# Key stores behind the first queries, exponents behind the taps, and a product on GpSimd in a two-layer hybrid encoder

## The chip, the cores and the metric

The kernel runs on one core of one Trainium2 chip. The time is the device time of one execution in microseconds (us). A core has five engines, each with its own instruction queue: PE (TensorE, matmuls; PEld is its weight load), DVE (VectorE), ACT (ScalarE), POOL (GpSimd) and SP (SyncE, which in this kernel only issues DMAs). An engine works through its queue in order, and an instruction that waits for a semaphore holds up everything behind it on its engine. L12 means line 12 of the kernel before the change.

## The reference

A trunk of two layers on 512 tokens with 1024 channels, in float32. Each layer adds half a SwiGLU block, a mixer, half a second SwiGLU block, and a gated embedding. The mixer of layer 0 is a bidirectional Mamba-2 scan (SSD), that of layer 1 a two-dimensional neighbourhood attention.

```python
for i in range(DEPTH):                                   # DEPTH = 2
    h = h + 0.5 * swiglu(rmsnorm(h, ffn1_norm[i]), ...)
    hn = rmsnorm(h, mix_norm[i])
    h = h + (ssd_mixer(hn, ...) if i % 2 == 0 else neighbourhood_attention(hn, ...))
    h = h + 0.5 * swiglu(rmsnorm(h, ffn2_norm[i]), ...)
    gate = sigmoid(rmsnorm(h, ple_norm[i]) @ ple_w_gate[i])
    h = h + gate * rmsnorm(p[i] @ ple_w_proj[i], ple_post_norm[i])

def ssd_mixer(h, ...):
    z, xbc, dt_raw = split(h @ w_in)
    xbc = silu(centred_depthwise_conv(xbc, conv_w, conv_b))      # 5 taps over the tokens
    xs, b_f, c_f, b_b, c_b = split(xbc)                          # forward and backward B, C
    dt = softplus(dt_raw + dt_bias)
    y = ssd_scan(forward) + flip(ssd_scan(flipped)) + xs * d_skip
    return rmsnorm(y * silu(z), norm_g) @ w_out

def ssd_scan(x, dt, a, b_mat, c_mat):                            # chunks of 128 tokens
    cum = cumsum(dt * a)
    scores = (c_mat . b_mat) * exp(lower triangle of cum[q] - cum[k])
    ...
```

In the attention, queries and keys are normalised per head, a block of 16 columns of queries sees a window of keys with a bias added, and the softmax weighs the values.

## The kernel before

Activations stay in SBUF, channels on the 128 partitions and tokens along the row (512 columns). A float32 product is made of three faster ones: each operand is split into a rounded high part and a residue, and `gemm` issues high by high (L278), activation residue or weight residue by high (L281, L282), in groups of three for each of the eight 128-channel blocks, 24 matmuls for one unit of 128 output channels. A weight unit comes by DMA into a `wr` tile, ACT casts it to `wh` (L221) and DVE makes its residue `wl` (L223). The tile framework's scheduler orders the instructions of each engine from the program and its own estimates, so an edit in one place can move instructions of others. `tc.issue_after(x)` keeps what stands under it behind instruction x.

**SSD** (`ssd`). First the eight normalised tiles `xn` are made: a product of the residual tile `hk[k]`, the gain and the row factor `R` (L687), and its split into high part and residue (L689, which ends in L303 on ACT and L304 on DVE; with a gain it would be L306 and L307). `project` then runs eight units for each of the eight groups of heads. The first three units of group 0 don't wait for `xn`: they use the unscaled tiles and multiply by R behind (L748). Each of the first six units of a group goes through `conv` (L742 to L760): one tap on ACT (L752), four on DVE (L756), a tanh on ACT (L759) and a last product on DVE (L760). `steps` (L690 to L739) makes the time steps and their cumulants, in which L716 on PE waits for L712 on DVE, and stores the cumulants as rows `crow` and `vrow` in HBM by sixteen small DMAs (L738, L739). `expo` (L789 to L805) loads a row of `crow` to all partitions and makes a tile of exponents with four Relus (L800) and four Exps (L803) on ACT. `scan` transposes and copies the group's inputs (L833), makes the products of C and B for both directions (`dr` 0 and 1; L841), masks them on DVE (L844), multiplies them by the exponents on POOL (L818, L821) and goes on to the outputs of a chunk and across chunks (L906, L909, L926, L929). While the scan of one group runs, the projection of the next does. PSUM has five banks for gemms (`mm_bank`) and three for the others (`px_bank`). Three exponent tiles of group 0 are issued right after its projection:

```python
e0 = [expo(0, j) for j in range(3)]
```

**Attention** (`attention`). Heads come in eight pairs. `keys` projects, normalises and splits the keys of four pairs at a time. A pair's keys are wanted "stacked": high part and residue of one head over one another. For pairs 0 and 1 this is done by DMAs from the split tile at once (`stack`, L1122: two DMAs each, four a pair); the others' keys go to HBM first (`kd`, L1189) and are stacked when their pair comes up. `project(j)` loads the pair's bias (L1204, L1205), projects the queries (L1212), splits them (L1216 on ACT, L1217 on DVE), stacks them by four DMAs (L1224), and makes the norms and the values (L1231, L1234, L1239). `attend(j)` makes the scores (L1255) from the stacked queries and keys, eight matmuls for half of the query blocks, adds the bias (L1265), takes exponents (L1272), and weighs the values (L1289, L1298, L1309). Pair 0's queries are projected while the keys of pairs 0 to 3 still go through normalisation and split.

```python
if js[0] + i < 2:
    stacked[js[0] + i] = [stack(kn.bitcast(F32), a) for a in range(2)]
    kz.append(None)
else:
    kd = dp.tile([P, 2, T], F32, name=nm("kd"))
    sy.dma_start(out=kd, in_=kn.bitcast(F32))
    kz.append(kd)
```

Of the kernel before, what the change touches and what calls it, by code (L numbers as in the profile page):

```python
# [14 lines left out]
P = 128  # L15
T = 512
# [54 lines left out]
def trunk(ctx, tc, A, out):  # L71
# [55 lines left out]
    def col(i):  # L127
        return cst[:, i:i + 1]
# [525 lines left out]
    def ssd(norm, nxt):  # L654
# [30 lines left out]
        for k in range(KD):  # L685
            t = t2()
            v.scalar_tensor_tensor(out=t, in0=hk[k], scalar=col(norm.gain + k), in1=R, op0=ALU.mult, op1=ALU.mult)  # L687
            xn.append(md(F32R))
            split(xn[k], t, None)  # L689

# [54 lines left out]
        def conv(src, ct, dst, raw):  # L745
# [5 lines left out]
            w = lambda j: ccw[:, j * 48 + ct:j * 48 + ct + 1]  # L751
            s.activation(out=a, in_=src, func=AF.Identity, scale=w(2), bias=ccw[:, 240 + ct:241 + ct])  # L752
            for j in (0, 1, 3, 4):
# [38 lines left out]
        def expo(gi, j):  # L792
# [12 lines left out]
            return e  # L805

        def scan(gi, bt, ct_, xt, zt, e0):

# [4 lines left out]
            def need(n):  # L813
                while len(es) <= min(7, n + (gi == 0)):
                    es.append(expo(gi, len(es)))

# [21 lines left out]
            for dr in range(2):  # L838
                pt = px_bank()
                for c in range(NC):  # L840
# [192 lines left out]
        for i, cur in enumerate(project(0)):  # L1033
            if i == 2:
                steps()
        e0 = [expo(0, j) for j in range(3)]

# [8 lines left out]
        for gi in range(NG):  # L1046
# [13 lines left out]
            for i, r in enumerate(beside):  # L1060
                cur = r
                while pending:

                    with tc.issue_after((row_cast if gi == NG - 1 else copied)[0].ins):
# [3 lines left out]
                        else:  # L1068
                            pending.pop(0)()

                for _ in range(count(gi, i)):
                    next(sn, None)
# [36 lines left out]
    def attention(norm, nxt):  # L1109
# [9 lines left out]
        def stack(src, a):  # L1119
            kt = md(F32R)  # L1120
            for x in range(2):
                sy.dma_start(out=kt[x * 64:(x + 1) * 64].bitcast(F32), in_=src[a * 64:(a + 1) * 64])  # L1122
            return kt

        def keys(js):
# [50 lines left out]
            for i in range(4):  # L1176
# [6 lines left out]
                split(kn, rb, None)  # L1183
                if js[0] + i < 2:
                    stacked[js[0] + i] = [stack(kn.bitcast(F32), a) for a in range(2)]
                    kz.append(None)
                else:
                    kd = dp.tile([P, 2, T], F32, name=nm("kd"))
                    sy.dma_start(out=kd, in_=kn.bitcast(F32))  # L1189
                    kz.append(kd)  # L1190
                if js[0]:
# [9 lines left out]
        def project(j):  # L1201
# [17 lines left out]
            for a in range(2):  # L1219
                r_ = slice(a * 64, (a + 1) * 64)  # L1220
                qt = bp.tile([P, T], F32R, name=nm("hs"), tag="hs", bufs=8)
                for x in range(2):
                    c_ = slice(x * 64, (x + 1) * 64)
                    sy.dma_start(out=qt[c_].bitcast(F32), in_=qs[x][r_].bitcast(F32))  # L1224
                qk.append((qt, stacked[j][a] if j < 2 else stack(kz[j], a)))
            yield
# [324 lines left out]
```

## Time and profile before

| | |
|---|---|
| Time, median of 3 runs (lowest to highest) | 2320.96 us (2320.68 to 2321.33) |
| Profiled execution: its own time | 2320.42 us |
| Profiled execution: its span, first to last instruction | 2318.6 us |
| Mean granted TensorE clock over the span | 0.998 of full speed |
| POOL busy | 324.3 us, 14% of the span |
| Data moved by DMA | 281.71 MB, 121 GB/s on average |

The profile is that of one execution. Its page gives the busy time of each engine, the chain of work that ended last, and the costliest groups of instructions; the trace behind it can be asked for the waits of an engine (who waited, for what, how long), for a timeline of single instructions, and for the busy time of each engine in chosen stretches. Idle time of an engine that nobody waits for costs nothing. In this span the SSD mixer's first group lies between about 360 and 480 us and the first attention pair between about 1700 and 1750 us.

### The profile page before, as it was taken

Reading aid. Unit: us, or ns where it says so; the run is one execution under the profiler, and the core shown is the slowest. Engines: PE = TensorE matmul, PEld = TensorE weight load, DVE = VectorE, ACT = ScalarE, POOL = GpSimd, SP = SyncE. Lnnn points to the kernel's source line nnn. Section 1 sums busy time; section 2 is a strip of 40 time slices with the busy share of each in tenths; the row PEclk is TensorE's granted clock in tenths of the full one; section 3 lists DMA queues with packets and bytes.
Section 4 is the critical chain, followed back from the end, with each engine's and each line's share of the span. In section 5 each row is a group of like instructions: output and inputs, shape, how many; then the busy total and the mean of one; then the engine's idle time right before and its main releaser. Section 6 shows DMA issues by size and latency. Waiting matters only on the chain.

```text
span 2318.6 us, 35451 instructions
## 1 busy us (share of the span) xinstructions
PE 2295.0 (99%) x13732; PEld 2026.4 (87%) x13732; DVE 1827.6 (79%) x2621; ACT 1178.5 (51%) x2038; POOL 324.3 (14%) x261
## 2 busy tenths in 40 slices
PE   9999999999999999999999999999989999999999
PEld 7899998788888888999998889999868888999987
DVE  7878868787788958987885898787569859878856
ACT  5434445777677764444445443444437654444452
POOL 0000001254455641000003100000210010000020
PEclk9999999999999999999999999999999999999999
DMA  5323323444444543333223233322457732333232
GB/s 187 118 77 109 105 88 130 136 164 138 145 138 152 185 159 118 105 103 103 100 74 104 101 107 100 101 89 83 166 169 207 222 117 95 110 105 101 84 94 73
DMA packets 105225, 281.71 MB, mean 121 GB/s; under 512 B 13136, under 2 KB 14032, under 8 KB 105056
## 3 DMA queue, kind: packets, MB, share of 16 engines
q1 hardware_dynamic: 104768, 279.30, 36.7%
q8 instruction: 108, 1.77, 0.3%
q14 instruction: 61, 0.50, 0.1%
q10 hardware_dynamic: 288, 0.14, 0.0%
HBM read 259.70 MB, written 13.40 MB: 118 GB/s over the span
## 4 chain that ended last, share of the span: by engine, by line
PE 92%; DVE 4%; ACT 1%; DMA 1%; issue 0%; SPq 0%; POOL 0%; ACTq 0%; DVEq 0%; POOLq 0%
PE ps L278 18%; PE ps L281 18%; PE ps L282 18%; PE ps L510 10%; PE ps L509 10%; PE ps L508 10%; PE ps L926 1%; DVE wl L223 1%; PE ps L885 1%; PE ps L1255 1%; DVE t L756 1%; PE ps L906 1%; PE ps L1309 1%; PE ps L1298 1%; PE ps L841 1%; DVE md L304 1%
## 5 line engine op out<-in xcount | busy, mean ns | idle before, releaser
L278 PE MATMUL ps<-md,wh 128*128 128x512 f32 (+1 forms) x2032 | 799.3, 394 | 1.1 <-DVE t L756 1.1
L282 PE MATMUL ps<-md,wl 128*128 128x512 f32 (+1 forms) x2032 | 790.8, 389 | 1.2 <-DVE wl L223 1.2
L281 PE MATMUL ps<-md,wh 128*128 128x512 f32 (+1 forms) x2032 | 791.7, 390 | 0.0
L221 ACT CAST wh<-wr 128x1024 fp32r<-128x1024 f32 (+2 forms) x395 | 351.7, 892 | 499.9 <-PE ps L281 258.5
L223 DVE TENSOR_TENSOR wl<-wr,wh 128x1024 fp32r<-128x1024 f32 (+2 forms) x395 | 418.2, 1060 | 84.4 <-ACT wh L221 82.7
L282 PEld LDWEIGHTS ps<-md,wl 128*128 128x128 f32 x2032 | 381.9, 188 | 83.2 <-DVE wl L223 2.7
L278 PEld LDWEIGHTS ps<-md,wh 128*128 128x128 f32 x2032 | 382.7, 188 | 75.6 <-issue 2.4
L281 PEld LDWEIGHTS ps<-md,wh 128*128 128x128 f32 x2032 | 382.8, 188 | 71.6
L221 ACT CAST wh<-md 128x1024 fp32r<-128x1024 f32 x175 | 183.6, 1049 | 321.8 <-PE ps L509 299.7
L332 POOL TENSOR_TENSOR sq<-sq,sq 128x512 f32<-128x512 f32 x71 | 101.0, 1423 | 1645.6 <-ACT sq L328 1641.2
L510 PE MATMUL ps<-sc,wl 128*128 128x256 f32 x980 | 277.4, 283 | 0.8 <-DVE wl L223 0.8
L508 PE MATMUL ps<-sc,wh 128*128 128x256 f32 x980 | 276.9, 283 | 0.8 <-ACT wh L221 0.8
L509 PE MATMUL ps<-md,wh 128*128 128x256 f32 x980 | 277.4, 283 | 0.1
L510 PE MATMUL ps<-md,wl 128*128 128x256 f32 x980 | 277.3, 283 | 0.0
L509 PE MATMUL ps<-sc,wh 128*128 128x256 f32 x980 | 277.3, 283 | 0.0
L508 PE MATMUL ps<-md,wh 128*128 128x256 f32 x980 | 277.1, 283 | 0.0
L514 DVE TENSOR_TENSOR t<-ps,t 128x512 f32<-128x512 f32 x245 | 165.9, 689 | 138.4 <-PE ps L510 137.8
L223 DVE TENSOR_TENSOR wl<-md,wh 128x1024 fp32r<-128x1024 f32 x175 | 213.5, 1220 | 16.6 <-ACT wh L221 16.3
L508 PEld LDWEIGHTS ps<-sc,wh 128*128 128x128 f32 x980 | 187.7, 192 | 4.9 <-ACT wh L221 1.0
L509 PEld LDWEIGHTS ps<-sc,wh 128*128 128x128 f32 x980 | 187.7, 192 | 3.9
L509 PEld LDWEIGHTS ps<-md,wh 128*128 128x128 f32 x980 | 188.0, 192 | 1.6 <-DVE md L472 0.4
L508 PEld LDWEIGHTS ps<-md,wh 128*128 128x128 f32 x980 | 188.0, 192 | 1.3
(209 smaller groups left out, 2898.3 us busy)
## 6 DMA issues: line engine op xcount, KB each, us to landing
wr<-in_w_gw_dram SPq DMA_DIRECT2D x70, 512.0 KB, 3.5
md<-in_w_gw_dram SPq DMA_DIRECT2D x70, 512.0 KB, 4.6
wr<-in_w_in_dram SPq DMA_DIRECT2D x65, 512.0 KB, 3.5
wr<-in_w_dn_dram SPq DMA_DIRECT2D x128, 256.0 KB, 2.6
wr<-in_w_gu_dram SPq DMA_DIRECT2D x32, 512.0 KB, 3.6
hs<-crow SPq DMA_DIRECT2D x64, 256.0 KB, 3.6
wr<-in_w_dn_dram SPq DMA_DIRECT2D x32, 384.0 KB, 3.0
wr<-in_w_qkv_dram SPq DMA_DIRECT2D x24, 512.0 KB, 3.7
```

Source lines behind the costliest of these rows:

```text
L221: splits.append(s.copy(out=hi[:, :n], in_=raw[:, :n]))
L223: v.tensor_sub(out=lo[:, :n], in0=raw[:, :n], in1=hi[:, :n])
L278: m = te.matmul(out=pt, lhsT=hi[:, sl], rhs=part(xp, 0, cols), start=first and k == 0, stop=False)
L281: te.matmul(out=pt, lhsT=hi[:, sl], rhs=part(xp, 1, cols), start=False, stop=False)
L282: gemm.last = te.matmul(out=pt, lhsT=lo[:, sl], rhs=part(xp, 0, cols), start=False, stop=last and k == n - 1)
L304: split.low = v.tensor_sub(out=dst[:, 1, :], in0=src, in1=dst[:, 0, :])
L332: (v if fast else g).tensor_add(out=self.acc, in0=self.acc, in1=q)
L508: te.matmul(out=o, lhsT=hi[:, sl], rhs=xh, start=j == 0 and kk == 0, stop=False)
L509: te.matmul(out=o, lhsT=hi[:, sl], rhs=xl, start=False, stop=False)
L510: te.matmul(out=o, lhsT=lo[:, sl], rhs=xh, start=False, stop=j == 1 and kk == 3)
L514: v.tensor_add(out=k[to], in0=pt, in1=k[other])
L756: v.scalar_tensor_tensor(out=a[:, lo:hi], in0=src[:, lo + o:hi + o], scalar=w(j), in1=a[:, lo:hi], op0=ALU.mult, op1=ALU.add)
```

## The change

It has four edits. In `ssd` the product for `xn` goes to POOL without the gain, and the split applies the gain. Of group 0's exponent tiles only the first is issued at once; the others are issued one at a time, each behind the latest ACT tap of `conv`. The C and B product of direction 0 takes a bank of the gemms' pool, in all groups. In `attention` the stacks of pair 1 and the stores of the keys of pairs 2 and 3 are put off until the first pair's query DMAs are issued.

```diff
@@ ssd
             t = t2()
-            v.scalar_tensor_tensor(out=t, in0=hk[k], scalar=col(norm.gain + k), in1=R, op0=ALU.mult, op1=ALU.mult)
+            g.tensor_mul(out=t, in0=hk[k], in1=R)
             xn.append(md(F32R))
-            split(xn[k], t, None)
+            split(xn[k], t, col(norm.gain + k))
@@ conv
-            s.activation(out=a, in_=src, func=AF.Identity, scale=w(2), bias=ccw[:, 240 + ct:241 + ct])
+            conv.tap = s.activation(out=a, in_=src, func=AF.Identity, scale=w(2), bias=ccw[:, 240 + ct:241 + ct])
@@ ssd
+        def spaced(j):
+            with tc.issue_after(conv.tap.ins):
+                return expo(0, j)
+
@@ scan
             def need(n):
                 while len(es) <= min(7, n + (gi == 0)):
-                    es.append(expo(gi, len(es)))
+                    es.append(spaced(len(es)) if gi == 0 else expo(gi, len(es)))
...
             for dr in range(2):
-                pt = px_bank()
+                pt = (mm_bank, px_bank)[dr]()
@@ ssd
-        e0 = [expo(0, j) for j in range(3)]
+        e0 = [expo(0, 0)]
...
+                if gi == 0 and i == 1:
+                    e0.append(spaced(1))
                 for _ in range(count(gi, i)):
                     next(sn, None)
@@ attention
+        unlaid = []
+
+        def lay(j, kn):
+            if j < 2:
+                stacked[j] = [stack(kn.bitcast(F32), a) for a in range(2)]
+            else:
+                kz[j] = dp.tile([P, 2, T], F32, name=nm("kd"))
+                sy.dma_start(out=kz[j], in_=kn.bitcast(F32))
@@ keys
-                if js[0] + i < 2:
-                    stacked[js[0] + i] = [stack(kn.bitcast(F32), a) for a in range(2)]
-                    kz.append(None)
+                j = js[0] + i
+                kz.append(None)
+                if j == 0 or j > 3:
+                    lay(j, kn)
                 else:
-                    kd = dp.tile([P, 2, T], F32, name=nm("kd"))
-                    sy.dma_start(out=kd, in_=kn.bitcast(F32))
-                    kz.append(kd)
+                    unlaid.append((j, kn))
@@ project
-                qk.append((qt, stacked[j][a] if j < 2 else stack(kz[j], a)))
+                qk.append((qt, stacked.get(j, [None] * 2)[a] or stack(kz[j], a)))
+            while unlaid:
+                lay(*unlaid.pop(0))
             yield
```

Three places show what it moves. The first is SP's queue at the first attention pair, before the change. L1122 are the stacks of pairs 0 (`md_16576`) and 1 (`md_16589`), L1189 the stores of keys, L1204 the bias and L1224 the stacking of the queries (`hs_16693`, `hs_16694` are their high part and residue).

```order
L1122 DMA md_16579<-md_16576 64x1024 x2
L1122 DMA md_16582<-md_16576 64x1024 x2
L1122 DMA md_16592<-md_16589 64x1024 x2
L1122 DMA md_16595<-md_16589 64x1024 x2
L1189 DMA kd_16605<-md_16602 128x1024
L1189 DMA kd_16614<-md_16611 128x1024
L1204 DMA md_16654<-in_bias_dram 128x1024
L1224 DMA hs_16697<-hs_16693 64x512
L1224 DMA hs_16697<-hs_16694 64x512
L1224 DMA hs_16700<-hs_16693 64x512
L1224 DMA hs_16700<-hs_16694 64x512
```

With the change the same queue reads as follows; lines are those of the changed kernel (L1128 stacks, L1138 stores, L1218 bias, L1238 queries).

```order
L1128 DMA md_16579<-md_16576 64x1024 x2
L1128 DMA md_16582<-md_16576 64x1024 x2
L1218 DMA md_16644<-in_bias_dram 128x1024
L1238 DMA hs_16687<-hs_16683 64x512
L1238 DMA hs_16687<-hs_16684 64x512
L1238 DMA hs_16690<-hs_16683 64x512
L1238 DMA hs_16690<-hs_16684 64x512
L1128 DMA md_16693<-md_16589 64x1024 x2
L1128 DMA md_16696<-md_16589 64x1024 x2
L1138 DMA kd_16699<-md_16596 128x1024
L1138 DMA kd_16701<-md_16603 128x1024
```

The four query DMAs moved ahead of the four stack DMAs of pair 1 and the two key stores.

The second place is DVE's queue in the front of SSD, up to the weight residue `wl_3916` of the fourth unit that uses `xn`; L708 and L709 belong to the time steps, the others to `conv`. Before the change:

```order
L708 SCALAR_TENSOR_TENSOR sc_3814<-sc_3814,sc_3813 128x256
L748 TENSOR_TENSOR t_3795<-ps_3764,rt_3648 128x512
L760 SCALAR_TENSOR_TENSOR md_3707<-t_3761,t_3755 128x512
L708 SCALAR_TENSOR_TENSOR sc_3814<-sc_3814,sc_3813 128x256
L756 SCALAR_TENSOR_TENSOR t_3797<-t_3795,ccw,t_3797 128x510
L709 SCALAR_TENSOR_TENSOR sc_3814<-sc_3814,sc_3812 128x256
L756 SCALAR_TENSOR_TENSOR t_3797<-t_3795,ccw,t_3797 128x511
L223 TENSOR_TENSOR wl_3916<-wr_3727,wh_3914 128x1024
```

And with the change:

```order
L748 TENSOR_TENSOR t_3795<-ps_3764,rt_3648 128x512
L760 SCALAR_TENSOR_TENSOR md_3707<-t_3761,t_3755 128x512
L708 SCALAR_TENSOR_TENSOR sc_3814<-sc_3814,sc_3813 128x256
L756 SCALAR_TENSOR_TENSOR t_3797<-t_3795,ccw,t_3797 128x510
L708 SCALAR_TENSOR_TENSOR sc_3814<-sc_3814,sc_3813 128x256
L756 SCALAR_TENSOR_TENSOR t_3797<-t_3795,ccw,t_3797 128x511
L708 SCALAR_TENSOR_TENSOR sc_3814<-sc_3814,sc_3813 128x256
L756 SCALAR_TENSOR_TENSOR t_3797<-t_3795,ccw,t_3797 128x511
L708 SCALAR_TENSOR_TENSOR sc_3814<-sc_3814,sc_3813 128x256
L756 SCALAR_TENSOR_TENSOR t_3797<-t_3795,ccw,t_3797 128x510
L708 SCALAR_TENSOR_TENSOR sc_3814<-sc_3814,sc_3813 128x256
L223 TENSOR_TENSOR wl_3916<-wr_3727,wh_3914 128x1024
```

All four taps (L756) of the unit whose bank is `ps_3764` now stand ahead of the residue, and the last step of the time-step polynomial (L709) behind it.

The third place is PE's queue around the cumulants (L716, L721, L733) of the time steps; `ps_3993` and `ps_4027` are the fourth and fifth unit that use `xn`. Before the change the cumulants stand in the fifth unit:

```order
L282 MATMUL ps_3993<-md_3703,wl_3916 128x512
L282 MATMUL ps_4027<-md_3668,wl_3956 128x512
L278 MATMUL ps_4027<-md_3673,wh_3954 128x512
L281 MATMUL ps_4027<-md_3673,wh_3954 128x512
L716 MATMUL ps_3833<-md_3659,msk 128x128 x4
L721 MATMUL ps_3840<-md_3659,ones_t 128x256
L282 MATMUL ps_4027<-md_3673,wl_3956 128x512
L733 MATMUL ps_3851<-msk,md_3659 128x128 x2
```

With the change they stand in the middle of the fourth:

```order
L278 MATMUL ps_3993<-md_3683,wh_3914 128x512
L281 MATMUL ps_3993<-md_3683,wh_3914 128x512
L282 MATMUL ps_3993<-md_3683,wl_3916 128x512
L716 MATMUL ps_3833<-md_3659,msk 128x128 x4
L721 MATMUL ps_3840<-md_3659,ones_t 128x256
L278 MATMUL ps_3993<-md_3688,wh_3914 128x512
L281 MATMUL ps_3993<-md_3688,wh_3914 128x512
L733 MATMUL ps_3851<-msk,md_3659 128x128 x2
L282 MATMUL ps_3993<-md_3688,wl_3916 128x512
```

The cumulants moved up by seventeen rows of PE's queue.

## The prediction

> **What bounds the kernel now.** I began with the page: its span, its busy shares and the summary of the chain that ended last.
>
> ```profile
> span 2318.6 us, 35451 instructions
> PE 2295.0 (99%) x13732; PEld 2026.4 (87%) x13732; DVE 1827.6 (79%) x2621; ACT 1178.5 (51%) x2038; POOL 324.3 (14%) x261
> PE 92%; DVE 4%; ACT 1%; DMA 1%; issue 0%; SPq 0%; POOL 0%; ACTq 0%; DVEq 0%; POOLq 0%
> ```
>
> TensorE (PE) is busy for 2295.0 of 2318.6 us, so all its idle time together is 23.6 us. The change removes no matmul. It can only win part of that idle time, or what PE loses at a lower clock. So the next view is the waits of PE, where each row has the waiting line, what it waited for, the total, the count and the longest wait. The row for L885 is from the same view of 360 to 480 us.
>
> ```profile
> PE ps L1255 <- DMA hs<-hs: 7.5, 1, 7.5
> PE ps L841 <- DVE sc L844: 2.2, 1, 2.2
> PE ps L282 <- DVE wl L223: 1.2, 2, 0.6
> PE ps L278 <- DVE t L756: 1.1, 1, 1.1
> PE ps L841 <- DVE sc L909: 1.1, 1, 1.1
> PE ps L926 <- DVE md L893: 1.0, 1, 1.0
> PE ps L885 <- POOL sc L857: 0.2, 1, 0.2
> ```
>
> The row of 7.5 us is the first pair's scores, which wait in attention for query tiles that come by DMA. One of the two 0.6 us waits for L223, and the waits of 2.2, 1.1, 0.2 and 1.0, stand in the front of SSD between 398 and 466 us, 5.1 us in all. The wait for L909 is in a later group of SSD. Third, I read the attention gap as a timeline (start, busy us, engine, line, count) and by windows (after the stretch's bounds: its length, then busy us and count of PE, PEld, DVE, ACT and POOL, then granted clock, DMA share and GB/s).
>
> ```profile
> 1726.69 2.28 PE L1255 MATMUL ps<-md,hs 128*128 128x256 f32 x8 [7.49 <-DMA hs<-hs]
> 1753.34 1.14 PE ps L1255 x8
> 1721.00:1722.00 1.00, 0.00 (x0) 0.00 (x0) 0.00 (x0) 0.00 (x0) 0.00 (x0) 0.64 1.04 426
> 1727.00:1731.00 4.00, 4.00 (x14) 3.36 (x14) 2.84 (x7) 0.29 (x1) 0.00 (x0) 0.50 1.01 399
> ```
>
> In the gap the clock falls, and it is 0.50 from 1727 to 1731: the eight score matmuls take 2.28 us there and 1.14 us in a later piece of the chain. So the wait costs more than 7.5 us. From 1726.69 to 1731 are 4.3 us of work at half speed, of which half is lost, 1.14 us on the eight alone, and the half clock ends a little after 1731: 2.3 us. **The place is worth 9.8 us.**
>
> **Attention, part by part.** Who makes the queries late? The rows are the makers of the queries (L1216, L1217), the last keys' residues (L304) and the DMA issues of SP.
>
> ```profile
> 1710.03 0.60 ACT L1216 CAST hs<-t 128x512 fp32r<-128x512 f32 x1
> 1710.67 0.69 DVE L1217 TENSOR_TENSOR hs<-t,hs 128x512 fp32r<-128x512 f32 x1
> 1718.52 1.28 DVE L304 TENSOR_TENSOR md<-sc,md 128x512 fp32r<-128x512 f32 x2
> 1705.87 9.74 SPq L1122 DMA_DIRECT2D md<-md  x8
> 1719.23 0.93 SPq L1189 DMA_DIRECT2D kd<-md  x2
> 1720.86 3.07 SPq L1224 DMA_DIRECT2D hs<-hs  x4
> hs<-hs SPq DMA_DIRECT2D x8, 128.0 KB, 3.4
> ```
>
> The queries were ready at 1710.67 + 0.69 = 1711.36, but their four issues begin at 1720.86, 9.5 us later. Ahead of them in SP's queue stand eight stack issues and two stores of keys (L1189), and the stores wait for keys whose residues end at 1718.52 + 1.28 = 1719.8. The changed SP order has only the four issues of the first pair's stack and one bias load ahead of the queries. The first stack is half of the 9.74 us group from 1705.87, so SP reaches the queries at about the time when they are ready. They go out from about 1711.4 to 1714 (3.07 us for four). With the median landing of 3.4 us of the issue table they are there near 1717, a little later if the loads around them crowd the queues. PE comes to its scores at 1726.69 - 7.49 = 1719.2. **The wait goes, with a margin of about 2 us.** With no gap there is no fall of the clock. What is late next is the softmax that hangs on the scores; its two waits stand there already.
>
> ```profile
> PE ps L1289 <- DVE sc L1265: 0.5, 1, 0.5
> PE ps L1298 <- DVE sm L1234: 0.8, 1, 0.8
> ```
>
> These follow the first scores at a fixed distance on DVE. PE's work between runs at full clock now, so they should be a little longer, 0.2 us together. The stacks of pair 1 and the two key stores go out behind the queries at about 1714 or, for the stores, when their keys are ready at 1719.8, as before; nobody reads pair 1 until after the first pair's scores. Sum: -7.5 - 2.3 + 0.2 = **-9.6 us**, with bounds -7.3 and -10.3.
>
> [...]
>
> **The front of SSD: the product on GpSimd.** After norm's end the eight xn tiles are made. Now DVE makes the product and the residue of each (L687, L304); afterwards GpSimd (POOL) makes the product and DVE a residue with the gain in it (L307). Their durations, alone and side by side:
>
> ```profile
> 369.05 2.72 DVE L687 SCALAR_TENSOR_TENSOR t<-hs,cst,rt 128x512 f32<-128x512 f32 x4
> 371.70 2.48 DVE L304 TENSOR_TENSOR md<-t,md 128x512 fp32r<-128x512 f32 x4
> 437.76 1.29 POOL L818 TENSOR_TENSOR sc<-sc,sc 128x512 f32<-128x512 f32 x1 [1.88 <-DVE sc L844]
> 800.44 4.93 POOL L935 TENSOR_TENSOR sc<-sc,hs 128x384 f32<-128x384 f32 x4 [15.35 <-DVE sc L909]
> 802.29 5.34 DVE L307 SCALAR_TENSOR_TENSOR md<-t,cst,md 128x512 fp32r<-128x512 f32 x4
> 367.82 0.59 ACT L359 COPY rt<-ps 128x512 f32<-128x512 f32 x1 [4.53 <-PE ps L356]
> 379.77 1.20 DVE L223 TENSOR_TENSOR wl<-wr,wh 128x1024 fp32r<-128x1024 f32 x1
> 381.64 0.39 PE L282 MATMUL ps<-md,wl 128*128 128x512 f32 x1
> ```
>
> On DVE the eight pairs cost 8 x (0.68 + 0.62) = 10.4 us. POOL takes 1.29 us a product alone, so eight would take 10.3 us and end a little before DVE does now. But the row at 802.29 shows the two engines in each other's way: four L307 take 5.34 us, 1.34 each instead of about 0.65, while POOL runs 384-element products beside them. The products here have 512 elements, which adds a quarter of 1.29 us, 0.32: 1.34 + 0.32 = 1.66, say 1.7 us for a product and a residue. The ends are 1.29 (no hindrance) and 1.29 + 0.65 = 1.94 (one after the other); I take 1.7 by the nearest row, since here too everything lies in SBUF.
>
> The factor is ready at 367.82 + 0.59 = 368.4. Two products go free, to 371.0; six pairs take 10.2 us, to 381.2; two residues remain, to 382.6. Then come one L748 (0.6 us, as long as a residue) and the first weight residue (L223, 1.2 us), which ends at 384.4 instead of 379.77 + 1.20 = 380.97. PE asks for this residue at 381.64. **A new wait of 2.8 us** (bounds: 0 with free products, 4.7 one after the other). No other engine is late for it: the cast of that weight on ACT stands behind the eight gain-scaled casts, and ends before DVE is there.
>
> From there PE and DVE both run without slack to the next late residue, that of the 0.6 us wait. Below are this wait, a piece of the chain (one matmul to the next, 0.23 us), and groups of DVE's instructions between 379 and 404 us (total and mean ns after the first bar).
>
> ```profile
> 399.20 0.50 PE L282 MATMUL ps<-md,wl 128*128 128x512 f32 x1 [0.62 <-DVE wl L223]
> 404.07 0.23 PE ps L281
> L708 DVE SCALAR_TENSOR_TENSOR sc<-sc,sc 128x256 f32<-128x256 f32 x6 | 2.5, 416 | 0.0
> L756 DVE SCALAR_TENSOR_TENSOR t<-t,ccw,t 128x511 f32<-128x511 f32 x6 | 4.4, 740 | 0.0
> L706 DVE TENSOR_SCALAR sc<-sc 128x256 f32<-128x256 f32 x1 | 0.3, 293 | 0.7 <-POOL sc L705 0.7
> ```
>
> DVE has 18.2 us of queue between the two residues (380.97 to about 399.2, when PE goes on). In the changed order two L756 are added and one L708 and the L709 drop out. Neighbours overlap by about 0.07 us, so this is 2 x 0.67 - 2 x 0.34 = +0.7 us: 18.9 us. PE needs 16.5 us (381.64 to 399.20, less its 0.62 us wait and two matmuls of 0.23 that no longer stand ahead): a wait of 2.4 us. DVE's own waits in that stretch, 0.7 for L705, may grow, since the time-step chain starts while DVE is late; by up to 1.0. I take 2.8 us (bounds 2.4 and 3.4) against 0.6 now.
>
> **The moved cumulants.** In the changed PE order L716 stands ten matmuls behind the first use of that residue; before it stood 25 rows behind it, past the use of the next residue. It waits for L712 on DVE, the eighth instruction behind the residue: L760, three L756 and four short ones (L708, L709, L711, L712), by the rows above and with the same overlap 0.6 + 3 x 0.67 + 4 x 0.34 = 4.0 us (L760 taken as long as a residue). PE's ten matmuls take 2.3 us. **A wait of 1.7 us** where none is now (bounds 0 and 2.3).
>
> **The exponents and the first scan.** Today three exponent sets (L800, L803) run on ACT in one piece, and the taps (L752) of three units queue behind them:
>
> ```profile
> 414.98 3.96 DMA hs<-crow
> 418.96 1.28 ACT sc L800 x4
> 427.61 0.68 ACT t L752
> 425.00:430.00 5.00, 5.00 (x31) 4.30 (x29) 1.71 (x4) 5.00 (x12) 0.00 (x0) 1.00 0.81 232
> ```
>
> ACT is busy for all of 425 to 430 while DVE works 1.71 of 5 us and falls behind; the waits of 2.2, 1.1, 0.2 and 1.0 us follow. With one set ahead and the others behind a tap each, this backlog goes and I count those four waits, and the 0.6, as removed: -5.1 us. But the first set still waits for crow, which lands later by what the front lost, and ACT's tanh (L759) stands behind two of its Relus. The bank of one unit behind it is freed only by the mask of the first C·B product, so I leave a wait of 1.2 us (bounds 0, and the present 2.2).
>
> The same edit gives the dr 0 product a bank of the gemm's pool in all eight groups. At 799 us it need no longer wait for L909; the bank that it now takes is freed earlier, by L929: half of the 1.1 us, -0.5 (bounds 0 and -1.1).
>
> Sum of SSD: 2.8 + 2.8 + 1.7 + 1.2 - 5.1 = **+3.4 us**, and -0.5 at 799. **All in all -9.6 + 3.4 - 0.5 = -6.7 us.** The profiled execution took 2320.42 us, 1.8 us around its span; the median is 0.54 us above it. So the median falls from 2320.96 to 2314.3.
>
> **Rivals.**
> First, the two engines don't hinder each other, because these products start two ahead: SSD is then 0 + 2.4 + 1.7 + 1.2 - 5.1 = +0.2, and with the last two hidden as well, -2.7. That gives 2311.1, down to 2308.2. Against it speaks the row at 802.29; for it, that ACT's casts stand between. Chance 0.24.
> Second, the queries are still late: they share the queues with stacks (256 KB each) and weights, and the windows of the gap show a DMA share of 1.0. If they land at 1721, 1.8 us remain: 2316.1. Chance 0.08.
> Third, the new stalls of 2.8 us cost clock. A stall of 2.2 us at 430 did not, the one in attention did after 2.1; each fall would cost up to 2.3 us as there: 2316.6 for one, 2318.9 for two. [...] Chance 0.12.
> Fourth, on the other side: the dr 0 product takes a gemm bank, so in each of groups 1 to 6 a unit of the projection waits until that bank is read. To end slower than before it would take 6.7 / 6 = 1.1 us in each group, for a measurable loss (below) 1.9. The mask that reads it (L844) is one DVE instruction of 512 columns, and PE has a whole unit of 24 matmuls (24 x 0.23 = 5.5 us) in between, so it decides only if DVE falls over 5 us behind. At 1.9 us each the time is 2325.6. Chance 0.04.
> That the change does not do what it says is out: the changed orders show each move.
>
> **How the numbers follow.** The forecast has 0.52, its own range is 2311 to 2317. A change of 0.2% (4.6 us) is what a measurement of this kernel can tell, so faster is below 2316.3 and slower above 2325.6. Faster: nearly all of the forecast (0.47), the first rival (0.24), a little of the second and third: 0.75. Slower: 0.03. The rest, 0.22, is the same. The terms' bounds are -10.3 to -7.3 for attention and -2.7 to +7.5 for SSD; with one of the two at its end and the other as taken, and with the third rival, the time lies from 2308.2 to 2318.9; 2308 to 2319 is the range.
>
> **What would show it.** Right: no wait of L1255 for a DMA, and a granted clock of 1.00 from 1715 to 1735; L307 and the new products alternating at about 1.7 us; waits of PE on L223 of 2 to 3 us twice near 382 and 400, on L712 near 403 of 1.7 us; no wait for L756, L893 in the first scan. Wrong: L307 at 0.7 us a piece beside POOL (then about 2311), L1255 still waiting for the queries, or a clock of 0.50 in the SSD front.

## The result and the profile after

| | before | with the change |
|---|---|---|
| Time, median of 7 runs each (lowest to highest) | 2320.96 us (2320.49 to 2321.81) | 2313.02 us (2312.72 to 2315.09) |
| Ratio, with its 95% interval | 1 | 0.9968 (0.9956 to 0.9979) |
| Span of the profiled execution | 2318.6 us | 2310.9 us |

By the medians the change makes the kernel faster by 7.9 us, 0.34% (0.32% by the ratio of the table); forecast were 6.7 us. The profile after has these totals on its page, and these waits of PE (in the changed kernel's lines L845 is the C and B product, L848 its mask, L1271 the scores, L1250 and L1294 DVE's parts of the norm and the softmax, L1305 and L1314 the matmuls behind them):

```profile
span 2310.9 us, 35433 instructions
PE 2294.1 (99%) x13732; PEld 2027.0 (88%) x13732; DVE 1828.3 (79%) x2613; ACT 1179.8 (51%) x2038; POOL 339.1 (15%) x269
```

```profile
PE ps L282 <- DVE wl L223: 2.8, 3, 1.5
PE ps L278 <- ACT wh L221: 1.8, 1, 1.8
PE ps L716 <- DVE md L712: 1.4, 1, 1.4
PE ps L1314 <- DVE sc L1294: 1.0, 2, 0.6
PE ps L1314 <- DVE sm L1250: 0.8, 1, 0.8
PE ps L278 <- DVE sc L848: 0.8, 1, 0.8
```

No row is left of the scores waiting for a DMA, nor of the four old waits of the first scan (L841, L756, L926, L885). New are the row for L221, that for L712, that for L848, and L1314 for L1294. POOL's busy time rose by 14.8 us; 12.7 us of it are the eight products.

To see where the time went I took the distances between the starts of marked matmuls in the two traces. In the front of SSD the marks are the time step's first transpose (L696) and the first transpose of group 1's scan; in attention they are the first scores of pairs 0 to 3 and, ahead of them, the first matmul of the keys' norms (L1168 before). All in us:

| stage | before | after | difference |
|---|---|---|---|
| front of SSD (380 to 477) | 95.76 | 98.10 | +2.34 |
| group 7 of SSD to the keys' norms | 887.12 | 885.86 | -1.26 |
| keys' norms to pair 0's scores | 42.25 | 34.60 | -7.65 |
| pair 0's scores to pair 1's | 20.35 | 17.93 | -2.42 |
| pair 1's scores to pair 2's | 18.96 | 19.95 | +0.99 |
| pair 2's scores to pair 3's | 18.50 | 19.22 | +0.72 |

These make -7.3 us; the rest of the -7.7 us of the span lies ahead of the mixer, whose first mark the changed kernel reached 0.5 us earlier (380.19 against 380.69). Attention won 10.07 us and gave 1.71 back in the next two pairs. SSD lost 2.3 us in its front and won 1.3 near 800 us.

**Attention.** PE's first scores and SP's queue in the timeline after the change, and then its windows (columns as in the prediction):

```profile
1719.59 1.11 PE L1271 MATMUL ps<-md,hs 128*128 128x256 f32 x8
1706.43 3.64 SPq L1128 DMA_DIRECT2D md<-md  x4
1710.11 0.58 SPq L1218 DMA_DIRECT2D md<-in_bias_dram  x1
1711.23 2.54 SPq L1238 DMA_DIRECT2D hs<-hs  x4
```

```profile
1721.00:1722.00 1.00, 1.00 (x6) 0.81 (x5) 1.00 (x4) 0.00 (x0) 0.00 (x0) 1.00 0.99 401
1722.00:1727.00 5.00, 5.00 (x28) 4.28 (x27) 4.45 (x13) 4.24 (x13) 0.00 (x0) 1.00 0.97 364
```

The scores follow their matmul without a wait and take 1.11 us instead of 2.28; the clock is 1.00 where it was 0.64 and 0.50. SP reaches the queries' DMAs at 1711.23, as reckoned (1711.4).

**The front of SSD.** The timeline after shows the product on POOL and what hangs on it, and a window the clock behind:

```profile
368.01 12.73 POOL L687 TENSOR_TENSOR t<-hs,rt 128x512 f32<-128x512 f32 x8 [10.75 <-ACT rt L359]
370.59 0.73 ACT L306 ACTIVATE md<-t,cst 128x512 fp32r<-128x512 f32 x1
372.29 0.72 ACT L306 ACTIVATE md<-t,cst 128x512 fp32r<-128x512 f32 x1 [0.97 <-POOL t L687]
373.99 0.73 ACT L306 ACTIVATE md<-t,cst 128x512 fp32r<-128x512 f32 x1 [0.98 <-POOL t L687]
379.84 1.45 DVE L307 SCALAR_TENSOR_TENSOR md<-t,cst,md 128x512 fp32r<-128x512 f32 x1 [0.24 <-ACT md L306]
381.52 0.75 DVE L307 SCALAR_TENSOR_TENSOR md<-t,cst,md 128x512 fp32r<-128x512 f32 x1 [0.24 <-ACT md L306]
382.48 0.50 PE L278 MATMUL ps<-md,wh 128*128 128x512 f32 x1 [1.83 <-ACT wh L221]
384.06 0.50 PE L282 MATMUL ps<-md,wl 128*128 128x512 f32 x1 [0.85 <-DVE wl L223]
```

```profile
385.00:388.00 3.00, 3.00 (x8) 2.31 (x7) 2.93 (x4) 0.03 (x1) 0.00 (x0) 0.50 0.73 250
```

A product and a residue take 1.70 us (ACT's casts stand 1.70 us apart, each waiting for POOL). A residue beside a product takes 1.45 us; the last one, when POOL is done, 0.75. So the two engines slow each other down, by the amount that the forecast took; the product on POOL takes 12.73 / 8 = 1.59 us here, against 1.29 alone. PE then waits twice, 1.83 + 0.85 = 2.7 us, and behind that the clock is 0.50 from 385 to 388. The whole stage by windows, before and after (first the length, then PE's busy time):

```profile
380.70:476.50 95.80, 90.72 (x452) 74.38 (x451) 79.65 (x111) 61.09 (x136) 22.30 (x20) 1.00 0.42 138
```

```profile
380.20:478.30 98.10, 91.77 (x452) 75.72 (x451) 81.47 (x114) 64.08 (x139) 24.97 (x21) 0.98 0.41 134
```

PE's idle time in the stage went from 95.80 - 90.72 = 5.1 to 98.10 - 91.77 = 6.3 us, and its busy time for the same 452 instructions rose by 1.05 us. The first is the exchange of old waits for new ones. In the second the half clock is more than 1.05: the eight matmuls from 384.65 to 388.04 took 3.39 us where at 0.23 us each they take 1.8, so it cost 1.6 us, and the rest of the stage was busy for 0.5 us less. These 1.6 us don't come on top of the waits. e4 below has the same queues up to about 430 us, and there the clock stayed at 1.00: PE came 1.6 us earlier to the next late residue and waited 3.0 us for it instead of 1.5.

### The profile page after: what moved, and what is told of

Same layout as the page of the kernel before. It is cut to its first block, busy times and chain, and to the rows that moved or that the text cites. A ratio compares the mean times of both kernels' runs of the same rounds, so it can differ in the third digit from the quotient of the medians.

```text
span 2310.9 us, 35433 instructions
## 1 busy us (share of the span) xinstructions
PE 2294.1 (99%) x13732; PEld 2027.0 (88%) x13732; DVE 1828.3 (79%) x2613; ACT 1179.8 (51%) x2038; POOL 339.1 (15%) x269
## 4 chain that ended last, share of the span: by engine, by line
PE 94%; DVE 3%; ACT 1%; DMA 1%; POOL 1%; issue 0%; SPq 0%; ACTq 0%
PE ps L278 19%; PE ps L281 19%; PE ps L282 19%; PE ps L510 10%; PE ps L509 10%; PE ps L508 10%; PE ps L930 1%; PE ps L889 1%; DVE wl L223 1%; PE ps L910 1%; PE ps L1325 1%; PE ps L1271 1%; DVE t L756 1%; PE ps L834 1%; POOL t L687 1%; PE ps L845 1%
## 5 line engine op out<-in xcount | busy, mean ns | idle before, releaser
L221 ACT CAST wh<-wr 128x1024 fp32r<-128x1024 f32 (+2 forms) x395 | 351.8, 892 | 491.7 <-PE ps L281 249.8
L221 ACT CAST wh<-md 128x1024 fp32r<-128x1024 f32 x175 | 183.6, 1049 | 322.6 <-PE ps L509 293.7
L510 PE MATMUL ps<-sc,wl 128*128 128x256 f32 x980 | 277.6, 283 | 0.8 <-DVE wl L223 0.8
L508 PE MATMUL ps<-sc,wh 128*128 128x256 f32 x980 | 277.0, 283 | 0.8 <-ACT wh L221 0.8
L510 PE MATMUL ps<-md,wl 128*128 128x256 f32 x980 | 277.4, 283 | 0.0
L508 PE MATMUL ps<-md,wh 128*128 128x256 f32 x980 | 277.2, 283 | 0.0
L508 PEld LDWEIGHTS ps<-sc,wh 128*128 128x128 f32 x980 | 187.7, 192 | 4.9 <-ACT wh L221 1.0
L508 PEld LDWEIGHTS ps<-md,wh 128*128 128x128 f32 x980 | 188.1, 192 | 1.3
```

The costliest lines, as they stand in the source:

```text
L221: splits.append(s.copy(out=hi[:, :n], in_=raw[:, :n]))
L508: te.matmul(out=o, lhsT=hi[:, sl], rhs=xh, start=j == 0 and kk == 0, stop=False)
L510: te.matmul(out=o, lhsT=lo[:, sl], rhs=xh, start=False, stop=j == 1 and kk == 3)
```

## The experiments

Each is given with its ratio to the kernel before on the same chip. The stages are those of the table above.

**e1: the attention edit alone.** The kernel before, with only the attention part of the change:

```diff
@@ keys
-                if js[0] + i < 2:
-                    stacked[js[0] + i] = [stack(kn.bitcast(F32), a) for a in range(2)]
...
+                if j == 0 or j > 3:
+                    lay(j, kn)
                 else:
+                    unlaid.append((j, kn))
@@ project
+            while unlaid:
+                lay(*unlaid.pop(0))
```

> The kernel before with the attention edit alone. Theory (the edit is worth 7.65 us of wait and 2.4 us of half clock, and 1.7 us of it come back as waits of L1314 near 1756 and 1775 because the edit itself reorders DVE there): 2320.96 - 10.1 + 1.7 = about 2312.6 us, with two later waits of 0.6 to 0.7 us that the kernel before doesn't have. Rival (the later waits come from the SSD edits or from chance): no such waits, about 2311 us.

Measured: 2313.2 us, ratio 0.9966 (0.9952 to 0.9979). The attention stages are those of the whole change to a few hundredths (34.60, 17.93, 19.93 and 19.21 us), and the later waits are there. So the edit itself brings them, and **the attention edit alone is worth as much as the whole change** (0.9968): within these intervals no gain or loss of the three SSD edits together can be told. In the front of SSD, which this kernel shares with the one before, the old wait of L841 was 2.9 us in this execution and 2.2 in that of before; the stage took 96.73 us in the one and 95.76 in the other: single executions differ by a microsecond there.

**e2: the product back on DVE**, with the other three edits.

```diff
@@ ssd, from the changed kernel
-            g.tensor_mul(out=t, in0=hk[k], in1=R)
+            v.scalar_tensor_tensor(out=t, in0=hk[k], scalar=col(norm.gain + k), in1=R, op0=ALU.mult, op1=ALU.mult)
             xn.append(md(F32R))
-            split(xn[k], t, col(norm.gain + k))
+            split(xn[k], t, None)
```

> The changed kernel with the residual's product back on DVE; the other edits stay. Theory (GpSimd and DVE hinder each other there, and the moved L716 is its consequence): the waits of 1.8 and 0.9 us near 382, the half clock behind them (1.6 us), the 1.5 us at 403 and the 1.4 us for L712 all go, while the old waits of 2.2, 1.1 and 1.0 us stay away: 2313.0 - 7 = about 2306 us. Rival (the old waits are gone only because PE came late and DVE could catch up): they come back, and the time is 2310 us or more.

Measured: 2307.37 us, ratio 0.9939 (0.9927 to 0.9951). The front of SSD takes 91.82 us instead of 98.10, and PE's waits between 360 and 480 us are these two:

```profile
PE ps L278 <- DVE sc L848: 1.4, 1, 1.4
PE ps L282 <- DVE wl L223: 0.6, 1, 0.6
```

The waits at 382, the half clock and the wait for L712 are gone, and the second late residue is back at the 0.6 us of before (L716 stands in PE's queue where it stood before the change). The old waits of the first scan do not come back, so it was not PE's lateness that hid them. The product on GpSimd, with the order of the queues that it brings, costs 6.3 us. The gain moves back with it, but that is little: a residue takes 0.75 us alone with the gain and 0.68 without. The theory was right, and 1.4 us too hopeful about the time: it had the 0.6 us for the residue go too, and the wait for the mask grew from 0.8 to 1.4 us.

**e3: the bank undone**, in the changed kernel.

```diff
-                pt = (mm_bank, px_bank)[dr]()
+                pt = px_bank()
```

> The changed kernel with both C and B products in the small pool of banks, as before. Theory (the wait of 1.27 us near 800 went because of the bank): it is back, about 2314.3 us; the 0.8 us wait of L278 for the mask in the first scan goes. Rival (the bank had no part in it): no wait near 800 and 2313 us or less.

Measured: 2314.96 us, ratio 0.9972 (0.9961 to 0.9983), whose interval overlaps that of the whole change. Near 800 a wait is back, but of 0.4 us by its row (0.6 from start to start), not 1.1; in e1, where the bank is also the old one, it is 0.5. In return the 0.8 us wait for the mask went. So the bank does remove the wait near 800, and what it brings there it takes in group 0, where the front is 97.48 us here and 98.10 with the whole change. These two stages cancel, so the traces give no reason for the 1.9 us between the two medians.

**e4: three exponent sets at once**, in the changed kernel.

```diff
-                    es.append(spaced(len(es)) if gi == 0 else expo(gi, len(es)))
+                    es.append(expo(gi, len(es)))
...
-        e0 = [expo(0, 0)]
+        e0 = [expo(0, j) for j in range(3)]
...
-                if gi == 0 and i == 1:
-                    e0.append(spaced(1))
```

> The changed kernel with the three first exponent sets issued at once, as before. Theory (the waits of 2.2, 1.1, 0.2 and 1.0 us came from the taps queued behind the exponents): ACT is busy in one piece again and these waits are back in most part, 3 to 4.5 us: about 2316.5 us. Rival (they went because PE was already late by the waits at 382 and 403): under 1 us comes back, 2313 to 2314 us.

Measured: 2320.3 us, ratio 0.9994 (0.9985 to 1.0003): nearly all of the change's gain is gone. The front takes 105.07 us, 7.0 more than with the exponents apart. Waits of PE between 360 and 480 us, two windows behind the stalls at 382, and one behind the wait for the taps:

```profile
PE ps L282 <- DVE wl L223: 3.9, 2, 3.0
PE ps L841 <- DVE t L756: 3.2, 1, 3.2
PE ps L278 <- ACT wh L221: 1.8, 1, 1.8
```

```profile
386.00:387.00 1.00, 1.00 (x6) 0.84 (x5) 1.00 (x2) 0.00 (x0) 0.00 (x0) 1.00 0.68 213
387.00:388.00 1.00, 1.00 (x7) 0.81 (x6) 0.96 (x2) 0.00 (x0) 0.00 (x0) 1.00 0.88 299
442.00:447.00 5.00, 4.22 (x14) 3.39 (x13) 4.06 (x7) 0.72 (x2) 2.60 (x3) 0.50 0.36 102
```

The theory holds, but its size was too small: the waits of the scan are back in another shape (3.2 us for the taps), and behind them the clock is halved from 441.1 to 447.9. Not all of the 7.0 us belong to the exponents, though. DVE, ACT and PE run the same queues as in the changed kernel up to about 430 us. There the stalls of 1.8 and 0.9 us left the clock at 1.00 (384 to 389), PE waited 3.0 us for the residue near 401, and the clock fell with this wait instead (0.79 in 403 to 404, 0.50 in each window from 404 to 407); when it was back, PE was 1.0 us behind the changed kernel, counted from the first mark. The other 5.9 us came behind 430 us, from the exponents. So spacing the exponents is the part of the SSD edits that wins.

**e5: rows of the later keys loaded early**, on top of e2.

```diff
@@ keys
             sy.dma_start(out=rkd, in_=rk[:8])
+            if js[0]:
+                rbs[0] = rows(0)
             yield
             for i in range(4):
-                rb = sc()
-                for a in range(2):
-                    ...
+                rb = rbs.pop(i) if i in rbs else rows(i)
...
                 if js[0]:
+                    if i < 3:
+                        rbs[i + 1] = rows(i + 1)
                     yield
```

> As the run with the product on DVE, and the row-factor loads of keys 4 to 7 are issued one step earlier (the first right behind the store of the factors, each other one behind the key before it). Theory (the two later waits of PE, 0.9 us for pair 1 and 0.6 us for pair 2, come from DVE's key product, which stands ahead of the softmax's work and waits 2.1 and 1.7 us for rows that SP issued only behind the next pair's queries): both go, 2307.4 - 1.7 = about 2305.7 us. Rival (the softmax chain itself is too long at full speed, and the rows only fill its time): the waits stay, 2307 us or more.

Measured: 2312.84 us, ratio 0.9963 (0.9950 to 0.9977): 5.5 us worse than e2. The rows came earlier and took the key product with them: it now stands in the softmax of pair 0. DVE's row of the key product (L1204 here), and two of PE's waits between 1710 and 1780 us:

```profile
1735.88 0.75 DVE L1204 SCALAR_TENSOR_TENSOR sc<-md,gqk,sc 128x512 f32<-128x512 f32 x1 [4.04 <-DMA sc<-rkd]
```

```profile
PE ps L1315 <- DVE sc L1291: 4.1, 1, 4.1
PE ps L1324 <- DVE sm L1260: 1.7, 1, 1.7
```

DVE waits 4.04 us for the rows ahead of the softmax's second half; the 4.1 us come from the keys' normalisation (L317 to L319, from 1723.8 to 1728.7), which DVE also took ahead of it. Pairs 1 and 2 are free of their waits (18.73 and 18.46 us). The expected time was missed, as the experiment moved the same blockade into the pair before instead of taking it away.

**e6: pair 1's stacks first**, on top of e2.

```diff
-                if j == 0 or j > 3:
+                if j < 2 or j > 3:
                     lay(j, kn)
```

> As the run with the product on DVE, but pair 1's keys are stacked at once, as before; only the two key stores go behind the first pair's queries. Theory (both parts of the new order count: four stack issues of 3.4 us stand ahead of the queries again, which then land near 1719.5 to 1721 counted as in the changed kernel): PE waits 0.5 to 2 us for the queries at its first scores, 2308 to 2309.5 us. Rival (only the stores that waited for late keys made the queries late): no wait for the queries, 2307.4 us.

Measured: 2312.13 us, ratio 0.9960 (0.9946 to 0.9974). SP's rows and PE's wait:

```profile
1700.85 9.71 SPq L1128 DMA_DIRECT2D md<-md  x8
1711.82 3.00 SPq L1238 DMA_DIRECT2D hs<-hs  x4
```

```profile
PE ps L1271 <- DMA hs<-hs: 3.9, 1, 3.9
```

Both halves of the new order count: with the stacks ahead 3.9 us of the 7.5 us are back, more than the 2 us expected, and with them 20.78 - 17.92 = 2.9 us of slower work behind (granted clock 0.50 from 1718 to 1724). The later waits are gone again (18.96 and 18.50 us). SP's order is again that of before here: the rows of the later keys go out at 1740.33, ahead of the next queries at 1746.93, and DVE waits for no row.

**e7: half of the products on GpSimd**, on top of e2.

```diff
-            v.scalar_tensor_tensor(out=t, in0=hk[k], scalar=col(norm.gain + k), in1=R, op0=ALU.mult, op1=ALU.mult)
+            if k % 2:
+                g.tensor_mul(out=t, in0=hk[k], in1=R)
+            else:
+                v.scalar_tensor_tensor(out=t, in0=hk[k], scalar=col(norm.gain + k), in1=R, op0=ALU.mult, op1=ALU.mult)
             xn.append(md(F32R))
-            split(xn[k], t, None)
+            split(xn[k], t, col(norm.gain + k) if k % 2 else None)
```

> As the run with the product on DVE, but four of the eight products (the odd ones, with the gain in the split) go to GpSimd. Theory (the two engines take turns there, so what GpSimd works is lost on DVE and more): DVE works 7.8 us and GpSimd 5.2 us, in turns 13.0 us instead of 10.4 us on DVE alone, so PE waits 1 to 2.5 us for the weight residue near 382, and the time is 2308.5 to 2310 us. Rival (the changed kernel's loss came from ACT's casts between the two, not from the two engines hindering each other): DVE is done 2.5 us earlier than with all on DVE, no wait near 382, 2307 us or less.

Measured: 2314.87 us, ratio 0.9972 (0.9962 to 0.9983). Rows of the two engines, with three products each beside one another (lines L688 and L690 here), and PE's waits between 360 and 480 us:

```profile
369.04 4.70 POOL L688 TENSOR_TENSOR t<-hs,rt 128x512 f32<-128x512 f32 x3 [10.75 <-ACT rt L359]
369.60 4.68 DVE L690 SCALAR_TENSOR_TENSOR t<-hs,cst,rt 128x512 f32<-128x512 f32 x3
```

```profile
PE ps L278 <- ACT wh L221: 3.6, 1, 3.6
PE ps L282 <- DVE wl L223: 3.1, 1, 3.1
```

These DVE products wait for no cast of ACT, and still take 4.68 / 3 = 1.56 us each, against 0.68 without a GpSimd neighbour. That settles the cause: the two engines slow each other, and ACT has no part in that. The expected place was wrong, though: there is no wait near 382. The scheduler put other weight work first, and PE's waits near 394 and 400 are for a cast and a residue that stand behind taps and time steps in the new queues of ACT and DVE, and the mean granted clock over the span was 0.997, where e2's was 1.000. So the time of this run is that of a new order and doesn't price the hindrance; the two rows of durations do show it.

**e8: the later keys a step later**, on top of e2.

```diff
-                if (j, n) == (0, 1) or n == 1 and 0 < j < 6:
+                if (j, n) in ((0, 1), (1, 1)) or n == 2 and 1 < j < 6:
                     next(far)
```

> As the run with the product on DVE, with the whole step of keys 4 to 7 (row loads, key product, split) one step of a pair later in the program. Theory (the two later waits of PE, 0.9 and 0.6 us, hang on DVE's key product waiting for its rows ahead of the softmax): with the product behind the first half's weighing the waits get shorter or go, 2306 to 2307 us. Rival (they are the softmax chain's own length): unchanged, 2307.4 us.

Measured: 2308.23 us, ratio 0.9945 (0.9931 to 0.9958), no better than e2. The two later waits (by their rows in e2 0.7 and 0.5 us) are gone, but six smaller ones at the scores, of 0.4 us at most, stand in pairs 1 to 4 instead (19.43, 19.50, 19.66 and 19.10 us a pair).

**e9: rows a step earlier, the product a step later**, on top of e2.

```diff
@@ keys
+                if js[0]:
+                    yield
                 v.scalar_tensor_tensor(out=rb, in0=raw[i], scalar=gqk, in1=rb, op0=ALU.mult, op1=ALU.mult)
@@ attention
-                if (j, n) == (0, 1) or n == 1 and 0 < j < 6:
+                if (j, n) in ((0, 1), (1, 1)) or n in (0, 2) and 1 < j < 6:
                     next(far)
```

> As the run with the product on DVE, with the row loads of keys 4 to 7 one step of a pair earlier and their product and split one step later. Theory: the rows are there before DVE comes to the key product, DVE waits for none, and the waits of PE of 0.9 and 0.6 us in pairs 1 and 2 go: about 2305.7 us. Rival (the softmax chain's own length): unchanged, 2307.4 us.

Measured: 2305.66 us, ratio 0.9932 (0.9920 to 0.9945). DVE's waits from 1720 to 1790 us have a row for the rows in e2, and none here:

```profile
DVE sc L1196 <- DMA sc<-rkd: 4.5, 3, 1.7
```

Pairs 1 and 2 take 18.94 and 18.46 us. So the 1.7 us that attention gave back were DVE standing still for rows ahead of the softmax, and they can be had. The intervals of e9, e10 and e11 overlap that of e2, so it is the stages that show these gains, not the times alone.

**e10: the old bank in group 0 only**, on top of e2.

```diff
-                pt = (mm_bank, px_bank)[dr]()
+                pt = mm_bank() if gi and dr == 0 else px_bank()
```

> As the run with the product on DVE, but in group 0 the C and B product of direction 0 keeps a bank of the small pool as before; the other groups take the gemms' bank. Theory (the 1.5 us wait of L278 for the mask in the first scan is the price of the bank there, and the wait near 800 belongs to group 7): the 1.5 us go, at most 0.4 us comes at the second product, the wait near 800 stays away: about 2306.2 us. Rival (the mask is late in any case, and L841's second product waits in its place): 2307.4 us.

Measured: 2305.67 us, ratio 0.9933 (0.9920 to 0.9945). The front takes 90.22 us instead of 91.82, and all that PE waits from 360 to 830 us is one row:

```profile
PE ps L282 <- DVE wl L223: 0.6, 1, 0.6
```

None of the old waits of the first scan is there, with the old bank: spacing the exponents is enough to remove them.

**e11: e2, e9 and e10 together.**

> The changed kernel with the three findings together: the product back on DVE, the bank of group 0 as before, the rows of keys 4 to 7 loaded a step earlier and their product a step later. Theory (the three gains lie in different stages and add up): the waits left of PE in the two stages are 0.8 us near 398 and 0.7 and 0.95 us in the first pair, and the time is 2307.4 - 1.6 - 1.7 = about 2304 us. Rival (a gain in one place is given back by an engine that is late in the next): 2305.5 us or more.

Measured: **2303.36 us**, ratio 0.9922 (0.9908 to 0.9935), the fastest of all. The gains add up in the stages: 90.20 us in the front, 17.93, 18.95 and 18.46 us for the pairs.

## Why the prediction was right, step by step

- **Attention, -9.6 us:** the wait went (7.65 us from start to start) and so did the half clock (2.42 us against 2.3 reckoned). SP's order was what made the queries late; e1 gives the gain of this edit by itself, and e6 shows both halves of the order at work. The term that was mis-sized is what comes back: +0.2 us was forecast for the two waits in the first pair. These stayed as they were, and 1.7 us came back in pairs 1 and 2 by another way (e1, e9): SP's new order has the next pair's queries ahead of the rows of the later keys (1745.72 and 1748.40 with the change; before, the rows went out at 1748.62 and the queries at 1755.22), and DVE waits for these rows ahead of the softmax. The forecast had only said that nobody reads pair 1 until after the first pair's scores, and had looked no further than what hangs on these.
- **Product on GpSimd:** 1.7 us for a product and a residue was forecast from one row of another stage, and 1.70 us was measured. The first wait was forecast with 2.8 us and measured with 1.83 + 0.85 = 2.7 us, most of it at the cast of ACT, which stands behind the eight gain-scaled casts; the forecast had it at the residue. The forecast had noted that this cast stands behind the others, but not that PE needs it as well. Behind the two stalls the clock was halved. This is the third rival, and a clock of 0.50 in this stage was one of the forecast's own signs of being wrong. Its price of up to 2.3 us did not come: by e4 the 1.6 us of slow work are taken off the next wait.
- **Second late residue, 2.8 us forecast:** 1.5 us behind half a clock, and 3.0 us in e4, where the clock was full up to there. So DVE was as late as forecast, and the small row of 1.5 is no sign of the contrary. The row for L705 is gone: on DVE two taps and L710 now stand between L703 and L706, which needs POOL's result.
- **Moved cumulants, 1.7 us forecast:** 1.4 us. **The mask's bank, 1.2 us:** 0.8 us.
- **Old waits, -5.1 us:** all five are accounted for; e2 and e10 show that spacing the exponents removes those of the scan, not PE's lateness or the bank. Without the spacing 5.9 us come back behind 430 us (e4), half clock included.
- **Near 800, -0.5 us:** 1.26 us went in the trace, but with the old bank the wait was 0.5 and 0.4 us in e1 and e3. So -0.5 is about the bank's part. The kernel before and e1 run the same SSD program, so the rest is a difference between single executions.
- **The sum of SSD**, +3.4 - 0.5 forecast, was +2.3 - 1.3. The new waits are 6.3 us instead of 8.5, and 1.6 us of half clock stand in the place of a part of them. So SSD was forecast too dear by 1.8 us, and attention too good by 1.2; another 0.5 us fell ahead of the mixer, where nothing was forecast. A part of the closeness is luck. What the sum did show, and what the runs bear out, is that the change wins in one place and about breaks even in the others, because the product on GpSimd eats what spacing the exponents brings.

## What to carry to other kernels

Before work is moved to a free engine, look in the trace for a place where the two engines run the same kind of operation side by side: GpSimd was 14% busy here, and work that it took from VectorE made both slower (a product on GpSimd 1.59 us instead of 1.29, a residue on VectorE 1.45 instead of 0.75), so that the pair took longer (1.70 us) than VectorE alone (0.68 + 0.62 = 1.30). In a queue that works in order, a DMA whose data are ready should not stand behind one whose data are not, nor behind several that nobody waits for yet (here PE waited 7.5 us for such DMAs); and when it is moved ahead, the next pass through the queue has to be looked at too, since here the same disorder came up in the next two pairs. A time that hardly moves can hide a gain and a loss of 6 us each, as that of the three SSD edits here: undo each part of a change alone.

## What the runs showed of the hardware

The clock of PE halved after stalls that were shorter than the one of 7.5 us in attention. In the changed kernel two stalls of 1.83 and 0.85 us within 3.4 us were followed by 0.50 from 385 to 388 us; in e4 one of 3.2 us by 0.50 from 442 to 447 us, and in e1, whose old wait was 2.9 us instead of 2.2, there was 0.50 as well:

```profile
433.00:434.00 1.00, 0.82 (x5) 0.82 (x6) 1.00 (x3) 0.13 (x1) 0.73 (x1) 0.72 0.63 184
434.00:436.00 2.00, 2.00 (x8) 1.81 (x8) 2.00 (x2) 1.17 (x2) 2.00 (x2) 0.50 0.40 160
```

PE was at work in these windows (0.82 and 2.00 us busy): here the halving hit the work behind the stall. What it cost depended on what came next. In attention before the change it cost 2.42 us; in the front of SSD its 1.6 us were taken off the next wait. Single stalls of 1.4 us (e2) and, in the profile before, 2.2 us went without it: the clock was 1.00 from 432 to 437 and from 430 to 435 us.

The length of the stalls alone does not decide. e4 has the same two stalls as the changed kernel, 1.8 and 0.9 us at the same matmuls, and kept the clock at 1.00 (384 to 389). The mean clock of a window between one at 1.00 and one at 0.50 gives the moment of change: 0.80 in 384 to 385 of the changed kernel means a fall at 384.6, and it was back at 388.0, 3.4 us later. In attention before the change, 0.64 in 1721 to 1722 means a fall at 1721.3, 2.1 us after PE ran out of work near 1719.2. By the same working the half clock lasted 3.4 us in e1 (433.4 to 436.8), 6.8 in e4 (441.1 to 447.9) and 10.2 in attention before (1721.3 to 1731.5). In the 3.4 us ahead of the fall PE stood idle for 2.1 us with the change, 2.1 in attention before, 2.1 and 2.8 ahead of the two falls in e4, and 2.9 in e1. So stalls of 2 to 3 us cost clock in some places and not in others: the two of 1.8 and 0.9 us did with the change and not in e4, one of 2.9 us did in e1, and the one of 2.2 us before did not. What decided it is not shown.

The matmuls on the split parts were the faster kind here: one with 128x256 results took 283 ns (L508 to L510 before), one of the same size on plain float32 380 ns (L721, L885).
